# Preparing the residual beside the last pair's products, and an even pace for the modulation beside the MLP

## The chip, the cores and the metric

The kernel runs on one core of one Trainium2 chip. The metric is the device time of one launch in microseconds, the median over runs. Engines are named as in the profile: PE (TensorE) multiplies, PEld loads its weights, DVE (VectorE) and ACT (ScalarE) do elementwise work, POOL (GpSimd) here mostly issues DMAs, SP issues most of the weight loads.

## The reference

One inference step through two post-norm layers over 128 context tokens and 512 latent tokens of width 1024, all in float32. Cut to what matters here:

```python
def trunk_layer(x, mod, p, ...):
    sh1, sc1, g1, sh2, sc2, g2 = jnp.split(mod, 6, axis=-1)
    u = x * (1.0 + sc1) + sh1
    m, ... = mixer(u, p, ...)
    x = layer_norm(ALPHA * x + g1 * m, p['ln1_g'], p['ln1_b'])
    h = x * (1.0 + sc2) + sh2
    f = jnp.square(jax.nn.relu(h @ p['w_up'])) @ p['w_down']
    return layer_norm(ALPHA * x + g2 * f, p['ln2_g'], p['ln2_b'])

for l in range(DEPTH):
    mod_ctx = silu(c_ctx) @ w_mod[l] + b_mod[l]     # for the context tokens
    mod_lat = silu(c) @ w_mod[l] + b_mod[l]         # for the latent tokens
```

The hidden width of the MLP is 4096. The modulation `mod` is a product of a vector with a 1024 x 6144 matrix for each of two kinds of tokens; it depends on the conditioning alone, so it can be worked out any time before it is used.

## The kernel before

**Precision.** Each float32 operand is split in a high and a low part (`act` copies the high part, `tt` subtracts it), and a product is three matmuls. So each weight that arrives is split by ACT and DVE before PE can use it.

**The MLP** of a layer goes in eight groups of 512 hidden columns (loop over `g`, L1451 on). Group 0 uses plain products; groups 1 to 7 compute their up products in two *fast pairs* each (`fast_pair`, L1328): seven part products of 12 matmuls with 320 columns in place of eight, on sums and differences of the tokens' halves (made once in `token_sums`) and of the weight's quarters: the four differences `t` (T1 to T4), which DVE makes and ACT and DVE split (`hi_T`, `lo_T`). The parts gather in the PSUM tiles px, pz and py; ACT copies some of them out (`s1`, `p5`, `u`), DVE adds, and `out` squares the relu and splits it into `ah`, `al`. Then ten down tiles of 128 tokens x 512 columns follow (`dn_block`). In layer 0 ACT copies each into `part`, and a DMA of POOL adds it to `acc`; in layer 1 DVE adds it. In what follows the up phase of a group is its two pairs, the down phase its ten down tiles.

**The last group.** `before_last` (L1432) runs once, in group 7: it empties the fillers (below), loads the gate's rows (`grow`, two DMAs of POOL into the slots of tag `ma`), and for each of five token tiles multiplies `acc` with the gate on DVE, loads the spilled `x` in two halves (DMAs of POOL) and adds `ALPHA * x` on DVE; then it has the norm's rows loaded (`norm_rows`, ACT's queue) and works out the next layer's `aff`. After that the last group's down tiles are added on top (`residual`), followed by the norm's statistics. In group 7 the tiles go token by token (`order`), and the first four are begun with half of their products.

**The modulation beside the MLP.** `mod_steps_sum` (L219) is a generator of *fillers*: for each piece (a sixth of a layer's modulation) it makes 16 steps, each with a load of 256 KB on POOL's queue (`ws`, three slots) and two multiply-adds into `ma` (DVE; for the first two of a piece ACT), and three steps of tail (`pmod` sums over partitions on PE, `mrow` out of PSUM, transposes `pmt`). With its first step that is 1 + 19 per piece. Layer 0's MLP holds six pieces (layer 0's last and five of layer 1's), layer 1's MLP one. `spread(n)` adds n to a counter and emits that many whole steps: `FU` at each output of a pair (eight per group), `FD` at each down tile (ten per group; none in group 7). `fill_all` emits all that is left.

**Order.** The program is traced in Python, and a planner then orders each engine's instructions at compile time, by a model of their times and by priority, which is the place in the program; `tc.high_priority(offset=-LATE)` puts instructions 100 places back. On the chip each engine works its list in order, and waits on semaphores. Tiles of one tag share a fixed number of slots: `flat` (L1252) hands out tag `u`, five slots, to the pairs' `t` and `p5` and to `before_last`'s `x`.

```python
        def flat(name):
            return op.tile([P, 4, P], F32, tag="u", name=name, bufs=5).rearrange("p a b -> p (a b)")
...
            s1, p5, u = room("s1" + nm), flat("p5" + nm)[:, :H], room("u" + nm)
            product(px, "B11", "A11")
            act(s1, px)
            product(pz, "T1", "S1")
            act(p5, pz)
            product(px, "T2", "S2", True)
            act(u, px)
            product(pz, "B22", "S4", True)
```

Of the kernel before, what the change touches and what calls it, by code (L numbers as in the profile page):

```python
# [8 lines left out]
F32 = mybir.dt.float32  # L9
# [7 lines left out]
P = 128  # L17
# [15 lines left out]

RK, RZ, RY, RS, RW = 4, 4, 1.5, 2, 1

FZ, FU, FD = 2, .6, 1.2

PIECES, PIECES_MLP = (2, 3, 4), (((0, 5),) + tuple((1, i) for i in range(5)), ((1, 5),))

# [2 lines left out]
LATE = 100  # L42
# [2 lines left out]

ORDERS, N_HALF = ((0, 1, 2, 3, 4), (4, 3, 0, 1, 2)), 4
NOTACT = (7,)


def bc(ap, dim, n):  # L50
# [8 lines left out]
def build(ctx: ExitStack, tc: tile.TileContext, I, O):  # L59
# [11 lines left out]
    def ps_tp(name):  # L71
        return pp.tile([P, 512], F32, tag="tp", name=name, bufs=2)
# [23 lines left out]
    def act(out, in_, func=AF.Copy, **kw):  # L96
        S.activation(out=out, in_=in_, func=func, **kw)  # L97
# [10 lines left out]
    def stt(out, a, s, b, op0, op1, **kw):  # L108
        V.scalar_tensor_tensor(out=out, in0=a, scalar=s, in1=b, op0=op0, op1=op1, **kw)  # L109

    def mm(out, l, r, start, stop):
        T.matmul(out, lhsT=l, rhs=r, start=start, stop=stop)  # L112
# [106 lines left out]
    def mod_steps_sum(pieces, pool):  # L219

        loads = [(l, pc, k, h) for l, pc in pieces for k in range(KT) for h in range(2)]
        got = {}

        def small(name):
            return pool.tile([P, 512], F32, tag="ws", name=name, bufs=3)

        def load():
            if loads:
                l, pc, k, h = at = loads.pop(0)
                w = got[at] = small(f"ws{l}_{pc}_{k}_{h}")  # L230
                c0 = pc * 1024 + h * 512
                G.dma_start(out=w, in_=I["w_mod"][l, k * P:(k + 1) * P, c0:c0 + 512])  # L232

        for _ in range(3):
            load()
        yield
        for l, pc in pieces:
            acc = [pool.tile([P, 1024], F32, tag="ma", name=f"ma{l}_{pc}_{s}", bufs=2) for s in range(2)]
            for k in range(KT):
                for h in range(2):  # L240
                    w = got.pop((l, pc, k, h))
                    with tc.high_priority(offset=-LATE):
                        for s in range(2):
                            a = acc[s][:, h * 512:(h + 1) * 512]
                            if k == 0:
                                act(a, w, scale=cst_c[:, k, s:s + 1])
                            else:
                                stt(a, w, cst_c[:, k, s:s + 1], a, ALU.mult, ALU.add)
                    load()
                    yield  # L250
            ps = ps_tp(f"pmod{l}_{pc}")
            for g in range(4):
                mm(ps[32 * g:32 * g + 32, :], one, acc[g // 2][:, (g % 2) * 512:(g % 2 + 1) * 512], True, True)
            yield from mod_tail(l, pc, ps, small(f"mrow{l}_{pc}"), False)
            yield
# [183 lines left out]

    def to_XT(name, pool, src, t, scale, bias, on_dve=NOTACT):  # L440

# [174 lines left out]
    for l in range(DEPTH):  # L616
# [621 lines left out]
        ng = 8  # L1238
# [86 lines left out]
                x = sp.tile([P, D], F32R, tag=f"S{len(made) - 3}", name=name)  # L1325
            return x[:, :3 * H].rearrange("p (i t) -> p i t", i=3)

        def fast_pair(g, j, ah, al):  # L1328

            i = 2 * j  # L1330
            nm = f"{l}_{g}_{j}"
            c0 = g * hg + i * P
            raw = []
            for k in range(2):
                r = raw_tile(f"rup{nm}_{k}").rearrange("p (k c) -> p k c", k=4)
                src = w_up[512 * k:512 * k + 512, c0:c0 + 256]
                nc.sync.dma_start(out=r, in_=src.rearrange("(k p) c -> p k c", p=P))
                raw.append(r)
            b11, b12, b21, b22 = (raw[k][:, :, P * c:P * c + P] for k in range(2) for c in range(2))
            w = {}  # L1340

            def unit(n, pool, bufs, t):
                return [pool.tile([P, n, 512], F32R, tag=x, name=f"{x}{nm}_{t}", bufs=bufs)
                        .rearrange("p i (k c) -> p i k c", k=4) for x in (("hi", "lo") if n == 2 else ("h1", "l1"))]

            b = unit(2, wp, 5, "b")
            for e, (n, x) in enumerate((("B11", b11), ("B21", b21))):
                act(b[0][:, e], x)
                tt(b[1][:, e], x, f(b[0][:, e]), ALU.subtract)
                w[n] = b[0][:, e], b[1][:, e]  # L1350
            t1, t2, t3, t4 = (flat(f"t{nm}_{i}").rearrange("p (a b) -> p a b", a=4) for i in range(4))
            sums = {"T1": (t1, b12, b11), "T2": (t2, b22, t1), "T3": (t3, b22, b12), "T4": (t4, b21, t2)}
            for ns in (("T2", "T1"), ("T3", "T4")):
                b = unit(2, wp, 5, ns[0])
                for n in sorted(ns):
                    tt(*sums[n], ALU.subtract)
                for e, n in enumerate(ns):
                    act(b[0][:, e], sums[n][0])
                    tt(b[1][:, e], sums[n][0], f(b[0][:, e]), ALU.subtract)
                    w[n] = b[0][:, e], b[1][:, e]  # L1360
            b = unit(1, op, 2, "c")
            act(b[0][:, 0], b22)
            tt(b[1][:, 0], b22, f(b[0][:, 0]), ALU.subtract)
            w["B22"] = b[0][:, 0], b[1][:, 0]

            def product(ps, wn, xn, more=False):

                for k in range(4):
                    wh, wl = (x[:, k] for x in w[wn])
                    xh, xl = quarter[xn](k)  # L1370
                    T.matmul(ps, lhsT=wh, rhs=xh, start=k == 0 and not more, stop=False, skip_group_check=more)  # L1371
                    T.matmul(ps, lhsT=wh, rhs=xl, start=False, stop=False, skip_group_check=more)  # L1372
                    T.matmul(ps, lhsT=wl, rhs=xh, start=False, stop=k == 3, skip_group_check=more)  # L1373

            def out(r, ct, half, src=None):
                spread(FU)
                o = H * half
                squared(r, ah[i + ct][:, o:o + H], al[i + ct][:, o:o + H], src)

            def bank(p, n):  # L1380
                return p(n + nm)[:, :H]


            px, pz, py = bank(ps_mm, "px"), bank(ps_tp, "pz"), ps_b2(f"py{nm}")[:, 0, :H]
# [8 lines that stand above are left out]
            tt(u, u, pz, ALU.add)  # L1393
            out(u, 1, 0)
            product(px, "T3", "S3", True)
            tt(p5, p5, px, ALU.add)
            out(p5, 1, 1)
            product(py, "B21", "A12")
            tt(s1, s1, py, ALU.add)
            out(s1, 0, 0)  # L1400
            product(px, "T4", "A22", True)
            out(room("c21" + nm), 0, 1, px)
# [29 lines left out]
        def before_last():  # L1432

            nonlocal rows
            fill_all()
            gate_rows(1)
            for t in order:
                a = acc[t]
                tt(a, a, grow[min(t, 1)], ALU.mult)
                for i in range(2):  # L1440
                    x, cs = flat(f"x{l}_{t}_{i}"), slice(i * 512, i * 512 + 512)
                    G.dma_start(out=x, in_=mid[l][t * P:(t + 1) * P, cs])
                    stt(a[:, cs], x, ALPHA, a[:, cs], ALU.mult, ALU.add)
            res[:] = acc
            rows = norm_rows(1)
            if l + 1 < DEPTH:
                make_aff(l + 1, 0, vt[:, 75:83], vt[:, 83:91])

        ends = []
        for g in range(ng):  # L1450
            ah, al = a_tiles(g, hg // P)  # L1451
            if g == 1:
                fillers.append(mod_steps_sum(PIECES_MLP[l], op))
            if g:
                for j in range(2):
                    fast_pair(g, j, ah, al)
                    if g == ng - 1 and j == 0:
                        before_last()
            else:
                for b in range(hg // 512):  # L1460
                    up_block(g, b, ah, al)
                    if g == 0 and b == 0:
                        with tc.high_priority(offset=-LATE):
                            for t, mv in later:
                                affine(rows, t, mv)
                                G.dma_start(out=mid[l][t * P:(t + 1) * P, :], in_=res[t])
                        rp_end.close()
                        sp, sp_end = open_pool("sp", "right")
                        with tc.high_priority(offset=-LATE):
                            token_sums()  # L1470
                token_sums_in_place()
# [108 lines left out]
```

## Time and profile before

| | us |
|---|---|
| median of 3 runs (lowest to highest) | 1635.98 (1634.4 to 1637.22) |
| the profiled execution's own time | 1634.55 |
| its span (first to last instruction) | 1632.7 |
| PE busy in the span | 1554.2 (95%) |
| DVE busy | 1221.5 (75%) |
| ACT busy | 885.4 (54%) |
| POOL busy | 171.5 (11%) |

The profile is one execution seen by the hardware profiler. Busy shares are averages over the span; PE's matmuls overlap at their ends, so its share says little about how fast it goes. What a place costs is read from its own stretch: who is idle there, and what ended the wait. Times inside the trace are microseconds from the span's start.

### The profile page before, as it was taken

How to read it: one execution, taken by the hardware profiler on the slowest of the kernel's cores; microseconds unless marked ns; L12 is line 12 of the kernel's file. 1: busy time of each engine (PE TensorE's matmuls, PEld its weight loads, DVE VectorE, ACT ScalarE, POOL GpSimd, SP SyncE). 2: the span in 40 equal slices, each digit the busy share in tenths (PEclk: the TensorE clock that was granted, in tenths of full speed). 3: DMA queues.
4: the chain of work that ended last, by engine and by line, in shares of the span. 5: the costliest groups of instructions: out<-in, count | busy, mean ns of one | idle time of the engine just before them, and what ended most of it. 6: DMA issues, size and time to landing. Idle time of an engine off the chain costs nothing.

```text
span 1632.7 us, 24085 instructions
## 1 busy us (share of the span) xinstructions
PE 1554.2 (95%) x8920; PEld 1358.1 (83%) x8920; DVE 1221.5 (75%) x2244; ACT 885.4 (54%) x1890; POOL 171.5 (11%) x274
## 2 busy tenths in 40 slices
PE   6999999999999999999598999999999999999997
PEld 3799957879889888878487999798798889988985
DVE  2588868869957686866787788898799665565677
ACT  3368744538556646545255577554486355434543
POOL 0000000001022242233200000000011000000011
PEclk9999999999999999999799999999999999999998
DMA  9641177343375786677535510524334232222332
GB/s 323 187 149 53 53 246 257 122 156 130 119 176 162 189 214 167 188 186 181 154 129 174 191 39 14 180 98 147 111 131 127 86 130 90 65 67 89 104 108 86
DMA packets 136518, 227.72 MB, mean 139 GB/s; under 512 B 12364, under 2 KB 73552, under 8 KB 136400
## 3 DMA queue, kind: packets, MB, share of 16 engines
q1 hardware_dynamic: 107632, 150.09, 28.7%
q0 software_dynamic: 21216, 57.68, 13.8%
q10 hardware_dynamic: 7552, 18.40, 3.2%
q8 instruction: 70, 1.15, 0.3%
q14 instruction: 48, 0.39, 0.1%
HBM read 191.95 MB, written 18.46 MB: 129 GB/s over the span
## 4 chain that ended last, share of the span: by engine, by line
PE 66%; DVE 12%; DMA 9%; issue 6%; ACT 5%; POOL 2%; SPq 0%; DVEq 0%; POOLq 0%; ACTq 0%
PE dn_t L112 17%; PE wo_t L112 5%; PE xb_c L112 4%; PE kv_t L112 3%; PE sa_c L112 3%; PE z_t L112 3%; PE px L1371 3%; PE px L1373 3%; PE px L1372 3%; DMA rup<-in_w_up_dram 3%; PE pt L112 2%; PE xa_c L112 2%; PE dq_t L112 2%; DMA ws<-in_w_mod_dram 2%; DVE ma L109 2%
## 5 line engine op out<-in xcount | busy, mean ns | idle before, releaser
L112 PE MATMUL dn_t<-hdn,al 128*128 128x512 f32 x640 | 252.1, 394 | 0.6 <-DVE al L100 0.6
L112 PE MATMUL dn_t<-ldn,ah 128*128 128x512 f32 x640 | 252.2, 394 | 0.0
L112 PE MATMUL dn_t<-hdn,ah 128*128 128x512 f32 x640 | 251.4, 393 | 0.3 <-ACT c L97 0.3
L109 DVE SCALAR_TENSOR_TENSOR ma<-ws,cstat,ma 128x512 f32<-128x512 f32 x196 | 138.8, 746 | 42.2 <-DMA ws<-in_w_mod_dram 32.3
L112 PEld LDWEIGHTS dn_t<-hdn,al 128*128 128x128 f32 x640 | 120.2, 188 | 29.7 <-issue 1.7
L112 PEld LDWEIGHTS dn_t<-hdn,ah 128*128 128x128 f32 x640 | 120.2, 188 | 28.6 <-ACT c L97 1.0
L112 PEld LDWEIGHTS dn_t<-ldn,ah 128*128 128x128 f32 x640 | 120.3, 188 | 26.8
L97 ACT ACTIVATE hi_T<-t 128x512 fp32r<-128x512 f32 x112 | 67.4, 626 | 64.0 <-DVE t L100 41.0
L100 DVE TENSOR_TENSOR ldn<-rdn,hdn 128x1024 fp32r<-128x1024 f32 x64 | 78.0, 1221 | 28.6 <-ACT hdn L97 28.5
L232 POOL DMA_DIRECT2D ws<-in_w_mod_dram x112 | 64.5, 579 | 276.1 <-DVE ma L109 183.3
L100 DVE TENSOR_TENSOR acc<-acc,dn_t 128x512 f32<-128x512 f32 x80 | 54.2, 684 | 49.5 <-PE dn_t L112 49.3
L100 DVE TENSOR_TENSOR lo_T<-t,hi_T 128x512 fp32r<-128x512 f32 x112 | 73.6, 684 | 22.5 <-ACT hi_T L97 22.3
L1371 PE MATMUL px<-XH,hi_T 128*128 128x320 f32 x224 | 72.5, 324 | 15.1 <-ACT u L97 8.2
L97 ACT ACTIVATE hdn<-rdn 128x1024 fp32r<-128x1024 f32 x64 | 67.1, 1052 | 18.4 <-PE px L1372 14.5
L97 ACT ACTIVATE hi_b<-rup 128x512 fp32r<-128x512 f32 x56 | 33.5, 623 | 77.7 <-PE dn_t L112 70.7
L97 ACT ACTIVATE part<-dn_t 128x512 f32<-128x512 f32 x60 | 35.4, 595 | 68.8 <-PE dn_t L112 47.6
L1373 PE MATMUL px<-XH,lo_T 128*128 128x320 f32 x224 | 70.9, 316 | 0.0
L1372 PE MATMUL px<-XL,hi_T 128*128 128x320 f32 x224 | 70.8, 316 | 0.0
L112 PE MATMUL wo_t<-hwo,XH 128*128 128x512 f32 x160 | 63.3, 395 | 1.9 <-ACT XH L97 1.5
L112 PE MATMUL wo_t<-hwo,XL 128*128 128x512 f32 x160 | 63.8, 399 | 0.0
L112 PE MATMUL wo_t<-lwo,XH 128*128 128x512 f32 x160 | 63.5, 397 | 0.0
L1486 POOL DMA_DIRECT2D acc<-part x60 | 53.1, 910 | 94.3 <-ACT part L97 83.3
(420 smaller groups left out, 4659.2 us busy)
## 6 DMA issues: line engine op xcount, KB each, us to landing
rup<-in_w_up_dram SPq DMA_DIRECT2D x64, 512.0 KB
rdn<-in_w_down_dram SPq DMA_DIRECT2D x64, 512.0 KB
ws<-in_w_mod_dram POOLq DMA_DIRECT2D x112, 256.0 KB, 3.7
acc<-part POOLq DMA_DIRECT2D x60, 256.0 KB, 4.3
wm<-in_w_mod_dram SPq DMA_DIRECT2D x24, 512.0 KB
Ab<-adram SPq DMA_DIRECT2D x10, 1024.0 KB
rwo<-in_w_out_dram SPq DMA_DIRECT2D x16, 512.0 KB
wb<-in_w_mod_dram SPq DMA_DIRECT2D x12, 512.0 KB
```

The costliest lines, as they stand in the source:

```text
L97: S.activation(out=out, in_=in_, func=func, **kw)
L100: V.tensor_tensor(out=out, in0=a, in1=b, op=op)
L109: V.scalar_tensor_tensor(out=out, in0=a, scalar=s, in1=b, op0=op0, op1=op1, **kw)
L112: T.matmul(out, lhsT=l, rhs=r, start=start, stop=stop)
L232: G.dma_start(out=w, in_=I["w_mod"][l, k * P:(k + 1) * P, c0:c0 + 512])
L1371: T.matmul(ps, lhsT=wh, rhs=xh, start=k == 0 and not more, stop=False, skip_group_check=more)
L1372: T.matmul(ps, lhsT=wh, rhs=xl, start=False, stop=False, skip_group_check=more)
L1373: T.matmul(ps, lhsT=wl, rhs=xh, start=False, stop=k == 3, skip_group_check=more)
L1486: G.dma_start(out=acc[t][:, cs], in_=part, accum_op=ALU.add)
```

## The change

`FU` goes from 0.6 to 1.15 and `FD` from 1.2 to 1. The three slots of `ws` get a name, `WS`, with the same value. `before_last` is no longer called after the first pair of group 7, but handed to the second pair, which calls it behind its operands' splits and ahead of its products, under `high_priority(offset=-LATE)`.

```diff
-FZ, FU, FD = 2, .6, 1.2
+FZ, FU, FD = 2, 1.15, 1
...
+WS = 3
...
-            return pool.tile([P, 512], F32, tag="ws", name=name, bufs=3)
+            return pool.tile([P, 512], F32, tag="ws", name=name, bufs=WS)
...
-        for _ in range(3):
+        for _ in range(WS):
             load()
...
-        def fast_pair(g, j, ah, al):
+        def fast_pair(g, j, ah, al, beside=None):
...
             act(b[0][:, 0], b22)
             tt(b[1][:, 0], b22, f(b[0][:, 0]), ALU.subtract)
             w["B22"] = b[0][:, 0], b[1][:, 0]
+            if beside:
+                with tc.high_priority(offset=-LATE):
+                    beside()
...
                 for j in range(2):
-                    fast_pair(g, j, ah, al)
-                    if g == ng - 1 and j == 0:
-                        before_last()
+                    fast_pair(g, j, ah, al, before_last if g == ng - 1 and j else None)
```

## Rows read from the trace of the kernel before

**Rows 1.** The page: busy tenths of PE and its granted clock, 40 slices.

```profile
PE   6999999999999999999598999999999999999997
PEclk9999999999999999999799999999999999999998
```

**Rows 2.** Layer 0's stretches: length, PE, PEld, DVE, ACT, POOL busy, clock, DMA share, GB/s.

```profile
437.80:463.90 26.10, 25.17 (x170) 24.64 (x169) 24.85 (x42) 16.06 (x33) 4.39 (x9) 1.00 0.60 181
...
491.90:518.30 26.40, 26.40 (x183) 25.30 (x182) 19.49 (x33) 19.04 (x39) 3.61 (x6) 1.00 0.54 152
...
716.50:747.50 31.00, 27.45 (x170) 27.16 (x169) 25.00 (x41) 15.98 (x33) 6.11 (x10) 0.89 0.66 184
747.50:777.60 30.10, 29.83 (x135) 22.92 (x134) 18.89 (x31) 15.95 (x32) 11.46 (x16) 1.00 0.77 182
777.60:828.80 51.20, 32.17 (x184) 29.18 (x183) 36.15 (x60) 17.14 (x35) 10.95 (x19) 0.77 0.56 168
828.80:859.00 30.20, 30.20 (x144) 24.53 (x143) 27.74 (x51) 18.01 (x34) 1.65 (x3) 1.00 0.24 83
```

**Rows 3.** Layer 1's stretches, same columns: a clean up and down phase, group 7's pairs.

```profile
1356.80:1381.40 24.60, 24.60 (x170) 24.60 (x169) 16.53 (x28) 16.73 (x34) 0.00 (x0) 1.00 0.32 107
1381.40:1408.90 27.50, 27.50 (x123) 22.57 (x122) 14.85 (x24) 7.41 (x15) 0.00 (x0) 1.00 0.20 58
...
1565.10:1593.50 28.40, 25.89 (x172) 25.01 (x171) 20.72 (x35) 15.67 (x33) 3.23 (x6) 1.00 0.42 138
```

**Rows 4.** Timeline of PE, 793 to 817: start, length, what, idle time before it.

```profile
793.18 0.64 PE L1371 MATMUL px<-XH,hi_T 128*128 128x320 f32 x1 [4.85 <-DVE p L100]
...
794.14 0.47 PE L1371 MATMUL px<-XH,hi_T 128*128 128x320 f32 x1
794.41 0.47 PE L1372 MATMUL px<-XL,hi_T 128*128 128x320 f32 x1
...
816.60 0.64 PE L1371 MATMUL pz<-Sh,hi_T 128*128 128x320 f32 x1 [14.14 <-ACT hi_T L97]
```

**Rows 5.** Timeline of DVE, 791 to 816.

```profile
791.99 0.74 DVE L109 SCALAR_TENSOR_TENSOR ma<-ws,cstat,ma 128x512 f32<-128x512 f32 x1
...
803.10 1.23 DVE L100 TENSOR_TENSOR acc<-acc,grow 128x1024 f32<-128x1024 f32 x1 [2.40 <-DMA grow<-gdram]
...
815.20 0.68 DVE L100 TENSOR_TENSOR t<-rup 128x512 f32<-128x512 f32 x1
```

**Rows 6.** Timelines of DVE, ACT and PE in group 6's up phase, 724 to 728.

```profile
724.22 1.41 DVE L109 SCALAR_TENSOR_TENSOR ma<-ws,cstat,ma 128x512 f32<-128x512 f32 x2 [0.84 <-DMA ws<-in_w_mod_dram]
...
726.27 0.63 ACT L97 ACTIVATE hi_T<-t 128x512 fp32r<-128x512 f32 x1 [5.58 <-DVE t L100]
...
727.27 0.64 PE L1371 MATMUL px<-XH,hi_T 128*128 128x320 f32 x1 [3.55 <-ACT u L97]
```

**Rows 7.** DVE by line, 777 to 829: count, busy us, mean ns, idle before.

```profile
L109 DVE SCALAR_TENSOR_TENSOR ma<-ws,cstat,ma 128x512 f32<-128x512 f32 x16 | 11.2, 747 | 4.0 <-DMA ws<-in_w_mod_dram 4.0
L109 DVE SCALAR_TENSOR_TENSOR acc<-x,acc 128x512 f32<-128x512 f32 x10 | 6.3, 680 | 0.0
L100 DVE TENSOR_TENSOR acc<-acc,grow 128x1024 f32<-128x1024 f32 x5 | 5.9, 1216 | 2.4 <-DMA grow<-gdram 2.4
...
L100 DVE TENSOR_TENSOR al<-u,ah 128x320 fp32r<-128x320 f32 x2 | 1.0, 493 | 2.1 <-ACT ah L97 2.1
```

**Rows 8.** Timeline of POOL: loads of x in layer 0 and in layer 1.

```profile
795.86 0.54 POOL L1442 DMA_DIRECT2D x<-mid  x1 [7.88 <-DVE al L100]
...
1551.69 1.14 POOL L1442 DMA_DIRECT2D x<-mid  x2 [219.96 <-DVE lo_T L100]
```

**Rows 9.** Stretches, instructions on ma alone: length, PE, PEld, DVE, ACT, clock, DMA.

```profile
437.80:463.90 26.10, 0.00 (x0) 0.00 (x0) 10.64 (x16) 0.00 (x0) 1.00 0.60 181
...
518.30:546.20 27.90, 0.00 (x0) 0.00 (x0) 13.43 (x20) 0.00 (x0) 1.00 0.83 214
...
716.50:747.50 31.00, 0.00 (x0) 0.00 (x0) 10.65 (x16) 0.00 (x0) 0.89 0.66 184
```

## The prediction

> **What bounds the kernel now.** I read the page's slices first: TensorE (PE) is nine tenths busy or more almost everywhere, and one slice in the middle, the twentieth, shows 5, with its granted clock at 7 [rows 1]. It is the end of layer 0's MLP. Next the stretches of that MLP, cut where PE goes from up products to down products and back [rows 2], beside the same stretches of layer 1, which has hardly any modulation to do there [rows 3]. Layer 1's clean phases are the floor: 24.6 us for two fast pairs, 27.5 us for ten down tiles, PE busy throughout. A piece's tail (eight pmod products and four transposes) adds 1.8 us: 26.4 in group 2's stall-free up phase less 24.6. Against this floor the seventh group's pairs of layer 0 take 51.2 us, 24.8 more than 24.6 + 1.8. PE is idle for 19.0 of them, and busy 5.8 us longer than it should be (32.2 against 26.4).
>
> PE's own rows [rows 4] show two idle times, 4.85 and 14.14 us, and what follows: products of 320 columns start every 0.27 us, where the floor phase has 168 of them in 24.6 us, one every 0.147: the lower level of the clock, 1.2 GHz, for some microseconds. The 5.8 us are mostly that. VectorE (DVE) shows why [rows 5]: until 792.7 it works off modulation (ma) which fill_all emitted in one lump, then it waits for grow, and from 803.1 to 815.2 it does before_last; only then comes the first difference t of the second pair, which PE is waiting for, through ACT's hi_T. So the place is bound by DVE's order, not by PE.
>
> Groups 1 to 6 of layer 0 take 339.8 us (437.8 to 777.6); at the floor they would take 6 x 52.1 + 5 x 1.8 = 321.6. The other 18 us are smaller stalls of one kind, worst in group 6, whose up phase is 31.0 us long [rows 2]: DVE waits for a ws transfer, its next t is late, ACT's hi_T waits 5.58 us for that t, the eviction of px stands behind hi_T on ACT, and PE is idle for 3.55 us [rows 6]. The modulation meant for the down phase had spilled into the next up phase.
>
> **The change, part by part.** (1) Pace. A piece is 19 filler steps (16 loads of 256 KB and 3 of tail), the generator 1 + 6 x 19 = 115. Before, a group emits 8 x 0.6 + 10 x 1.2 = 16.8 and pair 0 of group 7 another 2.4: 103, and fill_all has 12 left, nine loads, about 9 x 2 x 0.75 = 13 us of DVE [rows 7]. After, a group emits 8 x 1.15 + 10 x 1 = 19.2, six groups 115.2: fill_all finds nothing. The work is the same, moved earlier: 2.4 steps per group, 3.6 us of DVE. The 4.85 us and some 2.4 us of slow clock behind it go. WS is 3 as the number was: no cost.
>
> (2) before_last. It adds no instruction: 5 multiplies of 1.22 and 10 additions of 0.68 (they overlap: 12.2 us of DVE together), 2 grow and 10 x loads on POOL, 2 row loads on ACT [rows 7]. It moves behind the second pair's splits and 100 places back in priority, so t comes ahead of it; the 14.14 us and their slow clock go as such. What is late next? The x tiles, pair 1's four t and its p5 share five slots (tag u). POOL stood idle 220 us for layer 1's first x loads, though their data had long been there, until the splits of pair 0 gave up its t tiles, and the fifth x of layer 0 had to wait for pair 0's al, the last reader of p5 [rows 8]. So slots are handed out in the program's order, whatever the priority. After the change the order is t, ten x, p5: ACT can evict pz into p5 only when six x are used up, three tokens of the residual, 3 x 1.22 + 6 x 0.64 = 7.5 us of DVE and a second round of x loads. PE needs pz again after the third of pair 1's seven parts, each of twelve products: (84 + 36) x 0.147 = 17.6 us into the phase. DVE has by then pair 0's outputs (seven of 0.49 us [rows 7], 3.4), pair 1's splits (eleven of 0.68 us, as the t in [rows 5], 7.5), left-over modulation (up to 4) and the residual's 7.5: 18 to 22 us. This new wait costs 1 to 5 us and slow clock behind it; ACT's other work behind the waiting eviction is the pair's own. Its bounds are 0 (DVE starts early) and the old 14.14 + 3.4; I take 5 + 2 = 7, nearer to the DVE sum. So of 24.8 us some 18 are gained.
>
> The rest of before_last, about 5 us, falls beside pair 1's outputs, ldn and the last down phase, in which DVE is busy 27.7 of 30.2 us [rows 2]: little cover. Cost 0 to 6, taken 3. POOL's queue holds only group 6's accumulating transfers ahead of the x loads and no one's work behind them until the norms' pow; SP's queue is not touched; ACT's two row loads still wait for the last products that read the sums.
>
> (3) Groups 1 to 6. An up phase now gets 9.2 x 14/19 x 2 x 0.75 = 10.2 us of modulation beside some 16.5 of its own [rows 3]: 26.7 us of DVE in 26.4. It just fits. The nearest row is group 1's up phase: 16 ma instructions, 26.1 us long, 1.5 over the floor; group 6 did as many and took 31.0 [rows 2, 9]. A down phase gets ten steps for twelve, so less spills. If all six go like group 1 with half a microsecond for the down phase, the excess is 12 for 18, a gain of 6; if groups 2 to 6 go like group 6 (61.1 us), the stretch is 54.1 + 5 x 61.1 = 359.6, a loss of 19.8. I take a gain of 3, because the spill comes from the down phase, which is relieved.
>
> (4) Layer 1. Its generator has 20 steps and ends in group 2 either way. Its group 7 is 28.4 us now, some 3 over the floor [rows 3]; its second pair loses the old wait for t and gets the p5 wait, with 4 us less DVE work ahead of it: -3 to +3, taken 0.
>
> Sum: -18 + 3 - 3 + 0 = -18 us. The profiled execution is 1634.55 us (span 1632.7), which gives 1616.5; the median of the runs is 1.4 above it, so 1618.
>
> **The rivals.** All is hidden: DVE's free time in group 6's down phase lets the residual begin early, no p5 wait and no overflow, and groups 1 to 6 gain 6: -24.8 - 6 = -31, 1605. For it: DVE is busy only 18.9 of 30.1 us there [rows 2]; against it the order of the slots.
>
> It does not do what it says: the order of the slots keeps most of the residual ahead of pair 1's fourth product, so only the lump's 7.3 us and some 2 of the rest are gained: 1627.
>
> The transfers collide. The row: in group 2's down phase, with 20 ma instructions, the DMA engines are busy 0.83 at 214 GB/s [rows 9], and in group 6's 0.77 [rows 2]. 2.4 steps more per group are 2 loads, 0.53 MB, 2.5 us at that rate. If the queue were full, six groups would pay 15 us and gain no 3: -18 + 3 + 15 = 0, 1636. The Trainium skill, DMA: Bandwidth & Descriptors, section "Issuing engines are not separate DMA queues", speaks for this: transfers started by SP, ACT and POOL end on the same 16 engines and interleave, so POOL's faster ws loads would delay SP's weights. By that rule at a full queue it is 1636, by the row, which leaves a sixth free, nothing.
>
> Slower: the up phases, where DVE is full, cannot take twice the steps; the backlog lies in every group from 2 on and in group 7. Then +19.8, and of the 18 the 7 of the lump stay lost: -11 + 3 + 19.8 = +12, 1648. It decides when groups 2 to 6 are on average over 3 us longer than now. For it: groups 5 and 6 stall with 14 to 16 ma in the up phase; against it: group 1 with 16 does not.
>
> **How the numbers follow.** Forecast (1608 to 1630 by its bounds) 0.50, all hidden 0.14, slots 0.14, collision 0.07, slower 0.15. A measurement of this kernel can tell about 0.2%, 3.3 us. Faster 0.50 + 0.14 + 0.14 = 0.78, within 0.2% 0.07, slower 0.15. The range 1603 to 1638 takes in all but the slower case and the lower part of the hidden one.
>
> **What would show it.** Right: no ma instruction after some 782 us, the two idle times replaced by one of 2 to 8 us before pair 1's fourth product (pz) with ACT's p waiting for DVE or for an x; group 7's pairs 31 to 36 us long; clock near 1 there. Wrong: up phases of groups 2 to 6 over 29 us, or DVE full and PE idle from the last down phase to the next layer's first products.

## The result and the profile after

The changed kernel takes 1609.57 us (median of 4 runs, 1606.55 to 1611.66) where the kernel before takes 1636.6 beside it: a ratio of 0.9836, 95% interval 0.9817 to 0.9855, so 27 us or 1.6% faster. The forecast was 1618 in a range of 1603 to 1638. The profiled execution took 1609.03 us (span 1607.3), 25.5 less than that of before.

The page of the changed kernel, busy tenths and granted clock of TensorE in 40 slices, stands against [rows 1]:

```profile
PE   6999999999999999999999999999999999999997
PEclk9999999999999999999999999999999999999998
```

The hole in the twentieth slice is gone. Next the stretches, the answer to [rows 2] (length; PE, PEld, DVE, ACT, POOL busy and counts; granted clock, DMA share, GB/s): group 6's up and down phase, group 7's pairs and its down phase; then groups 1 to 6 as a whole, group 7 as a whole, and group 7 of layer 1.

```profile
719.60:745.50 25.90, 24.87 (x169) 24.60 (x168) 25.13 (x42) 16.77 (x34) 5.22 (x9) 1.00 0.72 203
745.50:775.20 29.70, 29.70 (x135) 23.08 (x134) 16.23 (x30) 13.15 (x26) 9.96 (x13) 1.00 0.77 180
775.20:806.70 31.50, 27.66 (x171) 26.41 (x170) 26.09 (x40) 15.19 (x33) 6.32 (x11) 0.95 0.69 220
806.70:837.10 30.40, 30.40 (x145) 24.73 (x144) 27.00 (x51) 18.01 (x36) 1.66 (x3) 1.00 0.17 55
...
440.10:775.20 335.10, 329.62 (x1804) 285.89 (x1803) 250.82 (x417) 191.12 (x376) 100.18 (x148) 1.00 0.74 192
775.20:837.10 61.90, 58.06 (x314) 51.14 (x313) 53.08 (x90) 33.21 (x67) 7.97 (x14) 0.97 0.43 139
1541.40:1596.00 54.60, 52.97 (x289) 46.97 (x287) 43.96 (x69) 28.72 (x62) 9.40 (x14) 1.00 0.35 116
```

The same three wholes of the kernel before:

```profile
437.80:777.60 339.80, 330.11 (x1792) 289.67 (x1791) 244.11 (x398) 190.11 (x375) 95.62 (x140) 0.98 0.71 182
777.60:859.00 81.40, 62.38 (x326) 53.71 (x325) 63.89 (x110) 35.15 (x68) 12.60 (x22) 0.85 0.44 137
1565.10:1621.50 56.40, 53.31 (x289) 46.70 (x287) 43.73 (x68) 29.66 (x62) 7.22 (x10) 1.00 0.27 94
```

Group 7 gave back 81.4 - 61.9 = 19.5 us, groups 1 to 6 4.7, layer 1's group 7 1.8. What group 7 still waits for stands in the timelines (start, length, engine, what, idle time before it and its end): PE, then ACT, then DVE and POOL.

```profile
799.20 0.42 PE L1376 MATMUL pz<-Sh,h_c 128*128 128x320 f32 x1 [3.36 <-ACT p L99]
...
801.05 0.47 PE L1376 MATMUL pz<-Sh,h_c 128*128 128x320 f32 x1
801.32 0.47 PE L1377 MATMUL pz<-Sl,h_c 128*128 128x320 f32 x1
...
798.71 0.44 ACT L99 ACTIVATE p<-pz 128x320 f32<-128x320 f32 x1 [3.49 <-DVE acc L111]
...
775.21 1.23 DVE L102 TENSOR_TENSOR acc<-acc,grow 128x1024 f32<-128x1024 f32 x1 [1.78 <-DMA grow<-gdram]
...
780.97 0.68 DVE L102 TENSOR_TENSOR t<-rup 128x512 f32<-128x512 f32 x1
...
792.50 0.69 DVE L111 SCALAR_TENSOR_TENSOR acc<-x,acc 128x512 f32<-128x512 f32 x1 [2.66 <-DMA x<-mid]
...
796.79 1.89 DVE L111 SCALAR_TENSOR_TENSOR acc<-x,acc 128x512 f32<-128x512 f32 x3
...
784.35 0.58 POOL L1447 DMA_DIRECT2D x<-mid  x1 [7.07 <-DVE lo_T L102]
```

The two idle times of [rows 4] have become one of 3.36 us, before pz, with ACT's eviction p waiting for an addition of the residual (the last of the three from 796.79, ended at 798.68); products at the lower clock (one every 0.27 us) follow. grow lies ready at 775 instead of 803, and pair 1's first t comes at 781 instead of 815 [rows 5].

### The profile page after: what moved, and what is told of

Same layout as the page of the kernel before. It is cut to its first block, busy times and chain, and to the rows that moved or that the text cites. A ratio compares the mean times of both kernels' runs of the same rounds, so it can differ in the third digit from the quotient of the medians.

```text
span 1607.3 us, 24073 instructions
## 1 busy us (share of the span) xinstructions
PE 1549.4 (96%) x8920; PEld 1352.1 (84%) x8920; DVE 1217.9 (76%) x2244; ACT 883.5 (55%) x1890; POOL 171.1 (11%) x274
## 3 DMA queue, kind: packets, MB, share of 16 engines
q8 instruction: 70, 1.15, 0.3%
## 4 chain that ended last, share of the span: by engine, by line
PE 59%; issue 15%; DVE 11%; DMA 8%; ACT 4%; POOL 3%; SPq 1%; POOLq 0%; DVEq 0%; ACTq 0%
PE dn_t L114 18%; PE xb_c L114 4%; PE kv_t L114 3%; PE z_t L114 3%; PE px L1376 3%; DMA ws<-in_w_mod_dram 3%; PE wo_t L114 3%; PE px L1378 2%; PE px L1377 2%; PE pt L114 2%; PE xa_c L114 2%; PE dq_t L114 2%; PE sa_c L114 2%; PE pmod L114 1%; PE sc L114 1%
## 5 line engine op out<-in xcount | busy, mean ns | idle before, releaser
L102 DVE TENSOR_TENSOR acc<-acc,dn_t 128x512 f32<-128x512 f32 x80 | 54.4, 684 | 52.2 <-PE dn_t L114 51.7
L99 ACT ACTIVATE pe<-sc,zs 128x640 f32<-128x640 f32 (+1 forms) x80 | 56.8, 712 | 7.4 <-DVE ams L108 3.0
```

The costliest lines, as they stand in the source:

```text
L102: V.tensor_tensor(out=out, in0=a, in1=b, op=op)
```

## The experiments

Each kernel ran beside its own runs of the kernel before (medians 1633.5 to 1635.4); ratios are to these. The theory that went in: the lump costs 7 us, the place of before_last costs the 14.14 us and its slow clock, and what is left is the wait for p5's slot. Its rivals: the two parts work on one chain; the slot is not the matter; the pace works by its sum alone.

**The pace alone.**

```diff
-fast_pair(g, j, ah, al, before_last if g == ng - 1 and j else None)
+fast_pair(g, j, ah, al)
+if g == ng - 1 and j == 0:
+    before_last()
```

> Only the pace of the change (FU 1.15, FD 1); before_last stays between the two pairs, as in the kernel before. Theory A, the terms add up: the lump's idle time of 4.85 us and its 2.4 us of slow clock go, groups 1 to 6 gain the 4.7 us that the changed kernel shows, the 14.14 us before pair 1 stay: 12 us faster than before, about 1624.5. Theory B, the two parts act on one chain: before_last's first multiply waited for grow from 792.7 to 803.1 because the lump's last sums had to pass pmod, the row and the load of grow; without the lump grow lies ready, so 10 of the 14.14 us go as well, and some slow clock behind them: about 24 us faster, near 1612, with one idle time of 3 to 6 us before the first t of pair 1.

1609.18 us, ratio 0.9856 (0.9833 to 0.988): all of the gain, without the move. **The move alone** (FU and FD back at 0.6 and 1.2):

> Only the move of before_last, behind the splits of pair 1 and 100 places back; the pace is the old one (FU 0.6, FD 1.2), so that fill_all still has its twelve steps, now beside pair 1. Theory A, the terms add up: the 14.14 us and 3.4 us of slow clock go, the wait for p5's slot comes (about 6 us): 12 us faster than before, near 1625, and groups 1 to 6 as before. Theory B, one chain: lump (13 us of VectorE), then 10 us until grow is there, then six additions of x, and only then p5's slot: the lump starts at about 785, grow comes near 810, p5 near 818, where TensorE wants pz near 796: some 20 us idle in one piece, no gain at all, 1632 to 1640.

1625.6 us, ratio 0.995 (0.9931 to 0.9968): 8 us less than the kernel before beside it, between the two expectations (12 us and none). **An even pace with the old sum**, so that a lump is left (the kernel with the pace alone, at FU 0.85 and FD 1):

> An even pace with the old number of steps: FU 0.85 and FD 1, 16.8 steps a group as before, before_last in its old place; some eleven steps are left for fill_all. It parts evenness from having done by group 6. Theory A (the gain in group 7 is the lump's, the gain in groups 1 to 6 is the even pace's): group 7's pairs stay at 48 to 51 us with an idle time of 10 us or more behind the wait for grow, groups 1 to 6 take 333 to 336 us: 1628 to 1631. Rival (all of it hangs on the pace beside the up phases): group 7's pairs 32 to 38 us, 1613 to 1618. Rival (evenness does nothing): groups 1 to 6 339 us or more, 1633 to 1637.

1625.83 us, ratio 0.9952 (0.9935 to 0.9969). The wholes of groups 1 to 6 and of group 7, same columns as above, in this order: pace alone (group 7 in two rows, pairs and down phase), move alone, even pace with a lump.

```profile
439.10:774.10 335.00, 329.78 (x1804) 286.03 (x1803) 251.07 (x418) 191.33 (x376) 100.15 (x148) 1.00 0.73 193
774.10:804.70 30.60, 27.54 (x172) 26.65 (x171) 25.17 (x40) 16.17 (x34) 6.30 (x11) 0.94 0.64 191
804.70:834.90 30.20, 30.20 (x144) 24.57 (x143) 27.70 (x51) 17.91 (x33) 1.65 (x3) 1.00 0.27 90
```

```profile
438.50:775.60 337.10, 328.99 (x1791) 288.49 (x1790) 244.75 (x399) 190.51 (x375) 95.83 (x140) 0.99 0.71 184
775.60:846.70 71.10, 60.44 (x326) 51.90 (x325) 60.85 (x107) 33.83 (x65) 12.65 (x22) 0.95 0.48 149
```

```profile
439.00:771.60 332.60, 327.41 (x1792) 287.32 (x1791) 246.13 (x399) 190.29 (x375) 96.05 (x140) 0.99 0.71 186
771.60:850.00 78.40, 60.96 (x326) 52.79 (x325) 62.43 (x108) 35.02 (x68) 12.02 (x21) 0.89 0.45 141
```

Group 7 takes 81.4 before, 60.8 with the pace alone (20.6 less), 71.1 with the move alone (10.3 less), 61.9 with both (19.5 less). The two gains don't add: with the pace in order the move adds nothing in group 7 (61.9 for 60.8). And an even pace without having done by group 6 leaves the big hole: the gain in group 7 is that of the missing lump. Groups 1 to 6, though, take 332.6 us there for 339.8 before, with no more steps than before: their gain there comes from how the steps are shared between up and down phases. Three timelines show the chain. With a lump and before_last in its old place, DVE first:

```profile
794.78 1.23 DVE L102 TENSOR_TENSOR acc<-acc,grow 128x1024 f32<-128x1024 f32 x1 [2.94 <-DMA grow<-gdram]
...
806.88 0.70 DVE L102 TENSOR_TENSOR t<-rup 128x512 f32<-128x512 f32 x1
...
808.29 0.63 PE L1376 MATMUL pz<-Sh,hi_T 128*128 128x320 f32 x1 [14.70 <-ACT hi_T L99]
```

With the pace alone, before_last in that same place:

```profile
773.93 1.23 DVE L102 TENSOR_TENSOR acc<-acc,grow 128x1024 f32<-128x1024 f32 x1 [1.57 <-DMA grow<-gdram]
...
791.38 0.69 DVE L102 TENSOR_TENSOR t<-rup 128x512 f32<-128x512 f32 x1
...
792.78 0.42 PE L1376 MATMUL pz<-Sh,hi_T 128*128 128x320 f32 x1 [2.68 <-ACT hi_T L99]
```

With the move alone, lump and residual beside pair 1:

```profile
795.43 2.20 DVE L111 SCALAR_TENSOR_TENSOR ma<-ws,cstat,ma 128x512 f32<-128x512 f32 x3
...
805.85 1.23 DVE L102 TENSOR_TENSOR acc<-acc,grow 128x1024 f32<-128x1024 f32 x1 [1.75 <-DMA grow<-gdram]
...
814.17 0.44 ACT L99 ACTIVATE p<-pz 128x320 f32<-128x320 f32 x1 [9.97 <-DVE acc L111]
```

The residual's 12 us of DVE begin when grow is there; in the three kernels with a lump that is 8 to 11 us after the last ma. Without the lump it is at 774 or 775. In the old place the whole residual is then done by 791, ahead of pair 1's t, for an idle time of 2.68 us; in the new place t comes at 781, and nine of the ten additions of x still lie behind 791. With the lump grow is there at 795 to 806: in the old place the residual then stands ahead of t, in the new one it holds p5's slot, and p waits 9.97 us for it. The expectation of 20 us idle for that case was too long: products of the down phase stand in the gap, and two idle times of pair 1 are left, 1.64 and 5.91 us, behind one of 2.16 in pair 0.

**Who waits for p5's slot.** First the allocation of p5 ahead of the call of before_last:

```diff
+s1, p5, u = room("s1" + nm), flat("p5" + nm)[:, :H], room("u" + nm)
 if beside:
     with tc.high_priority(offset=-LATE):
         beside()
```

> The changed kernel with one line moved: s1, p5 and u of the pair are allocated ahead of the call of before_last, so that p5 takes the slot of the pair's own t and the x tiles come behind it. Theory A (p5's slot is what pz waits for): the idle time of 3.36 us before pair 1's fourth product and the 2.4 us of slow clock behind it go in layer 0, up to 1.6 us in layer 1: 5 to 7 us faster than the changed kernel, near 1603. Rival (VectorE has too much to do there whatever the order): the idle time moves to the first product that needs VectorE's additions or to the last down phase, and the time stays within 2 us of 1609.6.

1609.36 us, ratio 0.9854 (0.9834 to 0.9874). In group 7 the engines do the same instructions in the same order, the wait included; ACT's row:

```profile
800.67 0.44 ACT L99 ACTIVATE p<-pz 128x320 f32<-128x320 f32 x1 [3.43 <-DVE acc L111]
```

So either the slot is not the matter, or slots are not handed out in the order in which the code allocates them. The next kernel parts these: x takes the slots of another tag, which nobody uses in group 7.

```diff
-x, cs = flat(f"x{l}_{t}_{i}"), slice(i * 512, i * 512 + 512)
+x = op.tile([P, 512], F32, tag="part", name=f"x{l}_{t}_{i}", bufs=3)
+cs = slice(i * 512, i * 512 + 512)
```

> The changed kernel with before_last's x tiles in the slots of the tag part (three of 512 columns, which the accumulating evictions of the groups before leave free in group 7) in place of tag u. Nothing else is changed; x and p5 no longer share slots. Theory A (x and p5 compete for tag u, whichever order the code allocates them in): ACT's p follows its u at once, near 795 in the changed kernel's times, the idle time of 3.36 us and 2.4 us of slow clock go, x loads start at 776 instead of 784: 5 to 7 us faster than the changed kernel, 1603 to 1605. Rival (VectorE is busy 26.4 of the 31.5 us and is the bound): TensorE waits for an addition of VectorE instead, 1608 to 1611.

1603.58 us (1601.83 to 1605.3), ratio 0.9821 (0.9805 to 0.9837). The changed kernel once more, for comparison:

> The changed kernel itself once more, as the measure for the run with x in tag part, beside the same runs of the kernel before: 1608 to 1611, the ratio 0.983 to 0.986. If it stands near 1604 as well, x's slots explain nothing; if it stands near 1609, they are worth 5 to 6 us.

1609.39 us (1605.93 to 1611.51), ratio 0.9849 (0.9827 to 0.9871). The intervals of the ratios overlap, but none of this kernel's four runs is as slow as the fastest of the changed kernel's eight; the medians are 6 us apart, the ratios 2.5 to 4.6 us. ACT, POOL, DVE and PE of layer 0's group 7 with x in part, then group 7 of both layers as wholes:

```profile
789.59 0.43 ACT L99 ACTIVATE p<-pz 128x320 f32<-128x320 f32 x1
...
771.16 0.89 POOL L1448 DMA_DIRECT2D x<-mid  x1
...
793.39 0.69 DVE L111 SCALAR_TENSOR_TENSOR acc<-x,acc 128x512 f32<-128x512 f32 x1 [2.03 <-DMA x<-mid]
...
798.40 0.41 PE L1376 MATMUL px<-XH,hi_T 128*128 128x320 f32 x1 [1.71 <-DVE p L102]
...
772.60:832.10 59.50, 56.74 (x314) 49.66 (x313) 52.59 (x90) 33.22 (x67) 7.38 (x13) 1.00 0.45 143
1536.60:1588.80 52.20, 52.20 (x289) 46.92 (x287) 41.11 (x63) 28.91 (x62) 4.82 (x6) 1.00 0.25 86
```

p no longer waits, x is loaded from 771 on instead of 784, and group 7 is 2.4 us shorter in each layer (59.5 for 61.9, 52.2 for 54.6); layer 1's has no idle time left. Slots are the matter, then, and not in the order of the code's allocations; that they go by the order that the planner makes is the reading left, not shown by a run of its own. What is left in layer 0 is DVE standing 2.0 us in front of an x, with u's and p's additions behind it. Six slots for x, in turn of tags part and ws:

```diff
-x = op.tile([P, 512], F32, tag="part", name=f"x{l}_{t}_{i}", bufs=3)
+x = op.tile([P, 512], F32, tag=("part", "ws")[i], name=f"x{l}_{t}_{i}", bufs=3)
```

> The changed kernel with the ten x tiles in six slots, turn by turn of tag part and of tag ws, which the modulation has left by then in layer 0: neither p5 nor the round trip of three slots holds them. Theory A (with x in part alone, what was left in group 7 was VectorE standing 2.0 us in front of an x while u's addition was queued behind it): that wait goes, TensorE's idle time of 1.7 us before pair 1's fifth product too, and the time is 1601 to 1603, 7 to 9 us under the changed kernel. Rival (three slots were enough): as the run with x in part, 1603 to 1605. If slots were not the matter at all, it stands at 1609.

1603.06 us (1600.22 to 1605.43), ratio 0.9819 (0.9798 to 0.9841). Its group 7 as a whole:

```profile
773.50:830.50 57.00, 56.21 (x314) 49.70 (x313) 52.76 (x90) 33.09 (x67) 6.84 (x12) 1.00 0.50 151
```

57.0 for 59.5: the wait and TensorE's 1.71 us are gone, but by the times the two kernels can't be told apart. With x in part, **before_last in its old place**:

> The new pace and x in tag part, but before_last in its old place between the pairs: the run with x in part less the move. Theory A (with the pace in order, the place costs what the residual puts ahead of pair 1's first t: the additions wait for x loads that now start earlier, so part of it goes): one idle time of 2 to 4 us before pair 1's first products, 3 to 5 us slower than the run with x in part, 1606 to 1609; then the move is worth these. Rival (the move is worth nothing, x's slots were all): 1602 to 1605.

1606.27 us (1604.56 to 1608.23), ratio 0.9833 (0.9813 to 0.9852). Group 7 takes 60.4 for 59.5, with idle times of 1.34 us before pair 0's last part (px) and 1.88 us in pair 1 (pz). By the medians the move is worth 2.7 us once x has slots of its own, by the ratios 2; the intervals overlap, so this is likely, not shown.

The other way to part p5 and x is **p5 in tag relu**:

```diff
-s1, p5, u = room("s1" + nm), flat("p5" + nm)[:, :H], room("u" + nm)
+s1, p5, u = room("s1" + nm), room("p5" + nm), room("u" + nm)
```

> The changed kernel with p5 in a slot of tag relu (four, of which a pair then uses all: s1, p5, u and c21) instead of tag u, in every pair. Theory A (the wait is for a slot of tag u): p no longer waits for the residual's additions; in group 7 it waits for a relu slot of pair 0, free near 793 to 795 by its al instructions: the 3.36 us go or shrink below 1, 3 to 6 us faster than the changed kernel, 1604 to 1607, unless the tighter relu slots cost every pair something: at 0.2 us a pair over 28 pairs 5.6 us, which would eat the gain. Rival (VectorE is the bound): 1608 to 1612.

1629.43 us, ratio 0.9978 (0.9964 to 0.9991): 20 us worse than the changed kernel, far outside both expectations. The loss lies in groups 1 to 6; DVE and PE in group 3's up phase, and the whole:

```profile
560.68 1.42 DVE L111 SCALAR_TENSOR_TENSOR ma<-ws,cstat,ma 128x512 f32<-128x512 f32 x2 [2.76 <-DMA ws<-in_w_mod_dram]
...
565.59 0.48 DVE L102 TENSOR_TENSOR u<-u,pz 128x320 f32<-128x320 f32 x1
...
567.85 0.64 PE L1376 MATMUL px<-XH,hi_T 128*128 128x320 f32 x1 [3.69 <-DVE p L102]
...
439.60:792.10 352.50, 336.01 (x1803) 294.04 (x1802) 253.71 (x421) 191.92 (x377) 101.05 (x150) 0.97 0.69 184
```

Each up phase of groups 1 to 6 got an idle time before a px (six, from 1.75 to 3.91 us), and group 7's pairs one of 3.49. DVE's order had changed: sums that wait for their ws stand ahead of u's and p's additions. That the tighter slots made the planner order it so is argued, not shown. On p5's slot this run agrees with x in part: in pair 1 of group 7 ACT's p follows PE, and PE no longer waits before pz.

```profile
813.22 0.44 ACT L99 ACTIVATE p<-pz 128x320 f32<-128x320 f32 x1 [0.52 <-PE pz L1378]
```

**The pace's two halves.** FU 0.6 with FD 1.52, then FU 1.65 with FD 0.6, both with the move:

> The changed kernel with an uneven pace of the same sum: FU 0.6 and FD 1.52, 20.0 steps a group for 19.2, so that fill_all still finds nothing; before_last as in the change. Theory A (my prediction's: what spills comes from the down phase): groups 1 to 6 go back to 340 us from 335.1, the time is 1614 to 1615. Rival 1 (only the sum per group counts): 1609 to 1611. Rival 2 (VectorE is full in the up phases, so steps belong beside the down phases): groups 1 to 6 take 332 or less, 1606.

1615.76 us, ratio 0.989 (0.9871 to 0.9909); groups 1 to 6 340.0 us.

> The changed kernel with the uneven pace the other way round: FU 1.65 and FD 0.6, 19.2 steps a group as in the change. Theory A (VectorE is the bound of an up phase): 13.2 steps there are 13.2 x 14/19 x 2 x 0.75 = 14.6 us of modulation beside 16.5 us of the pairs' own, 31 us in a phase of 26: groups 2 to 6 each 3 us longer, about 1625. Theory B (the loads of ws set how fast sums can be made, about 16 in an up phase, and the surplus runs over into a down phase with room): groups 1 to 6 335 to 338 us, 1609 to 1613. Theory C (what cost 5 us in the run with FD 1.52 was too many steps in the down phases, so the fewer the better): 1606.

1609.95 us, ratio 0.9856 (0.9838 to 0.9874); groups 1 to 6 338.1 us. And FU 1 with FD 1.15, on top of x in part:

> The run with x in tag part with the pace at FU 1 and FD 1.15, 19.5 steps a group for 19.2. Theory A (between FU 1.15 with FD 1 and FU 0.6 with FD 1.52 the time rises with the steps of the down phase): groups 1 to 6 take 335 to 337, 1604 to 1606. Rival (an up phase is short of VectorE, so fewer steps there help until the down phase spills): groups 1 to 6 332 to 334, 1601 to 1603.

1611.73 us, ratio 0.9862 (0.9843 to 0.9882), slower than both expectations; groups 1 to 6 339.4 us, group 7 62.5 for 59.5, with an idle time of 3.13 us before a px. Of seven profiles at FU 1.15 and FD 1 (without p5 in relu) six (the change twice, pace alone, p5 ahead, x in part, x in six slots) have 335.0 to 335.8 in groups 1 to 6, the seventh (x in part, old place) 333.3. So the sum alone doesn't do it: the two pairs with more steps in the down phases cost 4 to 5 us in these groups and lose time in the whole. The 3 us of FU 1.65 are open: its whole is not slower, and two profiles at the old pace, before and the move alone, are themselves 2.7 apart there (339.8 and 337.1). With FD 1.52 PE's two longest waits of the stretch are not for a px of the up phases, but before the tail's transposes (1.61 and 1.64 us; the second):

```profile
658.74 0.66 PE L170 MATMUL pmt<-ident,mrow 128*128 128x128 f32 x4 [1.64 <-ACT mrow L99]
```

With FD 1.15 PE's waits there are before px, for ACT's u and DVE's p (3.9 and 3.3 us in all), and before these transposes (2.3). Which of the two goes with which pace is not settled.

## Why the prediction was right, and where not

**Group 7's pairs: 18 predicted, 19.7 measured** (51.2 to 31.5). What is left above the clean 24.6 us [rows 3] is 6.9: 3.8 idle and 3.1 longer busy, for the 5 + 2 of the new wait. Of the 3.1 the lower clock is 1.4 (twelve products, each 0.12 us late); 0.5 are two products of the last down phase that PE does early. Place (pz), waiter (ACT's p) and releaser (the sixth of the residual's ten additions, ended at 798.68) are those of step (2). But p's slot is free only 23.5 us into the phase, later than the 18 to 22 of the sum, which adds up DVE's busy time alone: DVE also stands 2.66 us in front of the second x. The rest of the 19.7 is the piece's tail of 1.8, which the sum left in this stretch and which now lies in group 6's down phase.

**But the 14.14 us were put down to the wrong part.** Step (2) had them go because t comes ahead of the residual. The run with the pace alone shows that they go without that; the run with the even pace and a lump keeps 14.70. [rows 5] had the reason: DVE waits for grow until 803.1, and grow ends a chain from the last ma over pmod. SP and POOL of the kernel before:

```profile
513.47 0.68 SPq L184 DMA_DIRECT2D gdram<-mrow  x1
...
798.66 1.16 POOL L1148 DMA_DIRECT2D grow<-gdram  x2 [2.27 <-PE pmod L112]
```

The gate's row is the first of the six pieces and is written out at 513, so it is not the row that the lump holds back (as the expectation for the pace alone had it). grow takes the two slots of tag ma, and these are free when pmod has read the last sums. The lump's price was not 4.85 + 2.4 but nearly the whole of group 7's excess. That grow in slots of its own would have shortened the hole with the lump in place is likely, but no such kernel ran. That the sum came out is luck in this part: both parts are in the change, so it made no difference to the sum to which of them the 14.14 us were put; "it does not do what it says", 1627, would have been wrong for the same reason, since that case counted only 7.3 for the lump.

**The order of the slots.** "In the program's order, whatever the priority" is refuted, as the order of the code's allocations, by the run with p5 allocated ahead; that p5 waits for x's slots is confirmed by the run with x in part. [rows 8] shows a wait for slots, and no more.

**Overflow into the last down phase: +3 predicted, +0.2 measured** (30.40 for 30.20 [rows 2]). The last of the residual's ten additions ends at 803.2, before that phase begins; the term was sized as if 5 us of it fell into it.

**Groups 1 to 6: -3 predicted, -4.7 measured**, from 339.8; the move alone, at the old pace too, has 337.1, so 2 to 4.7. Group 6's up phase now has 17 ma instructions, 11.6 us of DVE, in 25.9 us; group 1's before had 16 in 26.1 [rows 9]. The reason given, that the spill comes from the down phase, is only half of it: the run with more steps there does lose 5 us, but before the tail's transposes as well as before px.

**Layer 1: 0 predicted; -1.8 in group 7 and -0.5 in groups 1 to 6.** The bound of -3 held.

**The rivals.** All hidden, 1605: its no-wait case needed other slots for x, which the change doesn't have; with them it is 1603.6. Collision: in groups 1 to 6 the DMA share rose from 0.71 to 0.74 and the stretch became 4.7 us shorter, so the 15 us of a full queue were not paid. The Trainium skill (DMA: Bandwidth & Descriptors, "Issuing engines are not separate DMA queues") states that DMAs of all issuing engines interleave on the same 16 engines; what that costs when these are full no run here shows. Overloaded up phases: the longest of groups 2 to 6 is 27.0 us, under the 29 named as the sign; even 13.2 steps an up phase (FU 1.65) gave 28.0 at most: no up phase there did more than 18 ma instructions, and the rest was done in the down phases.

The error of 7.5 us (-25.5 for -18 on the profiled execution) is thus 1.7 in group 7's pairs, 2.8 overflow, 1.7 groups 1 to 6 and 2.3 layer 1, less 1.0 outside the two MLPs: layer 0's MLP began 2.3 us later, and the stretch between the MLPs took 1.3 less. Over all the profiles that beginning lies between 437.5 and 440.8 whatever the edit, so it is not put down to the change.

## What to carry to other kernels

Where two edits aim at one hole, follow the hole's chain to its first link before sharing out its time: here the residual stood at the wrong place only because the row it needs was loaded late, into slots that the modulation still held, and the pace alone took the hole away but for 2.68 us. A tile that is moved past others competes with them for the slots of its tag: give it a tag that is idle there (4.8 us here in the two group 7's, 6 by the medians), and don't tighten a tag that every pair uses (20 us lost). And an in-order engine that waits for a load holds back everything behind it; look at what is queued there, not at its busy share.

## What was not expected of the hardware

What an idle time costs in clock does not follow its length. With the pace alone, 2.68 us of it were followed by about ten products at the normal pitch of 0.15 us and then by a dozen at 0.27, the lower level, from 794.9 to 798.2; these cost 1.4 us, and the stretch of the pairs has a granted clock of 0.94. After the changed kernel's 3.36 us it was 0.95, again with twelve such products. After the 14.14 us of the kernel before they were some 13, after group 6's 3.55 us [rows 6] 19. Shorter idle times went either way. With x in part and before_last in its old place, 1.34 and then 1.88 us left the clock at 1.00 throughout, as 1.71 us did with x in part and the move, and 2.16 us with the move alone. But with p5 in tag relu 2.47 us were followed by products at the normal pitch, and 1.86 us by twelve at 0.27:

```profile
509.45 0.41 PE L1376 MATMUL px<-XH,hi_T 128*128 128x320 f32 x1 [2.47 <-DVE p L102]
...
510.57 0.31 PE L1377 MATMUL px<-XL,hi_T 128*128 128x320 f32 x1
510.72 0.31 PE L1378 MATMUL px<-XH,lo_T 128*128 128x320 f32 x1
...
627.02 0.41 PE L1376 MATMUL px<-XH,hi_T 128*128 128x320 f32 x1 [1.86 <-DVE p L102]
...
629.58 0.47 PE L1377 MATMUL px<-XL,hi_b 128*128 128x320 f32 x1
629.85 0.47 PE L1378 MATMUL px<-XH,lo_b 128*128 128x320 f32 x1
```

So the length alone doesn't decide it here; what does is open.
